# The order in which the weight-load slots of the two expert layers are given out

## The chip, the cores and the metric

The kernel runs on one core of one Trainium2 chip. The time is the device time of one execution in microseconds (us); three runs give a median, and one further execution was profiled. The engines are TensorE (PE, with its weight loads PEld), VectorE (DVE), ScalarE (ACT), GpSimd (POOL) and SyncE (SP), whose queue issues nearly all weight loads.

## The reference, cut to what matters

Two networks of two layers each run one after the other on 256 tokens of width 1024 (the first carries 256 context tokens too). Everything is float32. In the first network each layer is a mixer (attention) and then a mixture of experts with 32 experts, of which every token uses two:

```python
for l in range(2):
    x (and ctx) = x + gate * mixer_l(modulate(norm(x)))        # mixer_ab in layer 0, mixer_c in layer 1
    tokens = modulate(norm(x))           # 512 tokens in layer 0 (ctx and x), 256 in layer 1 (x alone)
    group, expert = top1(tokens @ w_group), top2(tokens @ w_expert inside that group)
    for e in range(32):                  # w1, w3: 1024 x 512; w2: 512 x 1024
        y_e = (silu(t_e @ w1[e]) * (t_e @ w3[e])) @ w2[e]      # t_e: the tokens routed to e
    x = x + gate * sum of weight_e * y_e
```

The second network (sparse and latent attention, then a plain feed-forward) follows and is untouched.

## The kernel before

`body` runs `mixer_ab`, `moe(0)`, `mixer_c`, `moe(1)` and then the second network. An expert layer (`moe`) gives every expert 64 token rows; a rare second part (`overflow`, behind a branch on the largest count, L1325) takes what is over. It works on pairs of experts, sixteen pairs: `gather` builds the transposed tokens `xp` of four experts with one-hot matrices `G` (PE writes `tp`), `up` multiplies by w1 and w3 (PE writes `mm`, all through the helper `mm` at L1024), `turn` transposes the gated product (L1248), `down` multiplies by w2, `weigh` scales (DVE, ACT, L1279 to L1281), and `scatter` adds the rows back into `x` (L1295).

All 32 experts' weights pass through SBUF once: 32 x 3 x 2 MB in each layer, as loads of 128 x 1024 floats (512 KB), 12 for each expert, 384 in a layer. Each load goes into a **slot**. `raws` (L295) asks `slot` for the next one and issues the load with `late` (L185), which keeps it in program order on SP's queue. SP works its queue strictly in order: a load that must wait for its slot's memory holds back all behind it.

Slots come from three places. The ring buffers that the mixers use for their own weights (6 `raw`, 3 `wh`, 3 `wl`, written `b` in the tables) serve as 12 slots. Tiles of the mixers that are dead by then serve as well: `r0` to `r3` are the mixer's attention output (in layer 1 the tiles `oT` that `mixer_c`'s last product reads), and `r6`, `r7` the residual rows of the context, which layer 1 no longer needs after `mixer_c`'s norm at its start. The rest is memory of the mixer's own pools, which close when it ends: `x0`, `x1`, ... at the front of that region and `y0`, `y1`, ... behind the layer's own tiles. Layer 0 has 4 x and 2 y (with 4 r and 12 b: 22 slots), layer 1 has 8 x and 5 y (31 slots). In what order they go out in a lap is a table, one string for each layer:

```python
order = order.split()
order += [k for k in (*extra, *once) if k not in order] + ["b"] * (len(base) - order.count("b"))
lap = [(k, base.pop(0) if k == "b" else extra.get(k)) for k in order]
self.rings["raw"] = [e for k, e in lap if e]
self.lap = [new.get(k) or once.get(k) or e for k, e in lap]
```

The first lap takes the entries of `self.lap`; later laps repeat the same order. In the first lap a load waits until the mixer's last access to the memory under the slot is done, in later laps until PE has read what lay in it. The mixer's end is in SP's way like this: the router's `logits` are the mixer's last step (L976 on ACT writes squares into a tile `pr` of the closing pools, L421 on POOL ends the norm's factor), and `x0` of both layers lies over memory that this step uses. The loads of the mixer's own weights (L319, `w_out_ab`, `w_out_c`; split into `wh` and `wl` at L327 and L330) stand ahead of the expert loads in SP's queue.

At the end of a layer `ahead` loads the first weights of what follows into the `raw` ring (for layer 1 three loads of `w_in_2`), before the branch L1325.

Of the kernel before, what the change touches and what calls it, by code (L numbers as in the profile page):

```python
# [25 lines left out]
def shape_constants():  # L26
# [32 lines left out]
    for dim in (64, 32):  # L59
# [21 lines left out]
PTE = "avav"  # L81

MOE = ((4, 2), (8, 5))
MJ = ("r0 r1 r2 y0 y1 x0 x1 x2 x3 b b b b r3 b b b b b b b b",
      "x0 x1 x2 x3 b b b b r0 r1 r2 r3 b b x4 x5 x6 x7 r6 r7 b b b b b b y0 y1 y2 y3 y4")
AH = ("ap", "ap")

CP = dict(s=2, tp=3, o=1, pa=2)
# [30 lines left out]
class Kern:  # L119
# [877 lines left out]
    def moe(self, l, whos, ahead=list):  # L997
# [16 lines left out]
        free |= {f"y{i}": (more, f"y{i}", 1) for i in range(MOE[l][1])}  # L1014
        self.slots(first, MOE[l][0], order=MJ[l], free=free)
        gates = []
# [948 lines left out]
```

## Time and profile before

| | |
|---|---|
| median of 3 runs | 2349.37 us (2348.11 to 2349.89) |
| profiled execution | 2353.45 us, its span 2351.7 us |
| busy in the span | PE 2181.2 us (93%), DVE 1119.8 (48%), ACT 780.7 (33%), POOL 345.9 (15%) |
| moved by DMA | 593.12 MB, mean 252 GB/s |

Busy time is that of the profiled execution's span, which leaves out 1.75 us of that execution's time. Matmuls are pipelined and their ends are modelled, so PE's busy time counts waiting inside the pipeline too. The page also cuts the span into 40 slices of 58.8 us with the busy share of each engine and the DMA rate in them; layer 0's experts lie in slices 6 to 14, layer 1's in slices 19 to 27.

### The profile page before, as it was taken

Reading aid. Unit: us, or ns where it says so; the run is one execution under the profiler, and the core shown is the slowest. Engines: PE = TensorE matmul, PEld = TensorE weight load, DVE = VectorE, ACT = ScalarE, POOL = GpSimd, SP = SyncE. Lnnn points to the kernel's source line nnn. Section 1 sums busy time; section 2 is a strip of 40 time slices with the busy share of each in tenths; the row PEclk is TensorE's granted clock in tenths of the full one; section 3 lists DMA queues with packets and bytes.
Section 4 is the critical chain, followed back from the end, with each engine's and each line's share of the span. In section 5 each row is a group of like instructions: output and inputs, shape, how many; then the busy total and the mean of one; then the engine's idle time right before and its main releaser. Section 6 shows DMA issues by size and latency. Waiting matters only on the chain. (4 is left out here: it accounts for less than half of the span.)

```text
span 2351.7 us, 32726 instructions
## 1 busy us (share of the span) xinstructions
PE 2181.2 (93%) x12405; PEld 1391.2 (59%) x12405; DVE 1119.8 (48%) x2251; ACT 780.7 (33%) x1585; POOL 345.9 (15%) x478
## 2 busy tenths in 40 slices
PE   5999989999999998998899999999899999899998
PEld 3865564444444437986433333333667998767997
DVE  4565664434343347766312122221566654666654
ACT  3444542111111115655201110110555443655443
POOL 1621120000000003443000000000323110232111
PEclk8999999999999999999899999999989999989999
DMA  8467639999999983220999999999433652425561
GB/s 290 134 226 270 220 113 367 381 387 387 387 387 386 387 303 114 77 72 9 357 387 387 386 387 387 386 387 383 152 126 116 230 178 99 160 84 169 188 207 37
DMA packets 306785, 593.12 MB, mean 252 GB/s; under 512 B 25270, under 2 KB 57020, under 8 KB 306620
## 3 DMA queue, kind: packets, MB, share of 16 engines
q1 hardware_dynamic: 305436, 587.68, 70.3%
q10 hardware_dynamic: 1184, 3.27, 0.4%
q8 instruction: 100, 1.64, 0.3%
q14 instruction: 65, 0.53, 0.1%
HBM read 589.82 MB, written 1.05 MB: 251 GB/s over the span
## 5 line engine op out<-in xcount | busy, mean ns | idle before, releaser
L330 POOL TENSOR_TENSOR wl<-raw,wh 128x1024 fp32r<-128x1024 f32 (+1 forms) x17 | 41.4, 2439 | 1148.8 <-SPq L1325 529.7
L1239 ACT ACTIVATE hs<-mm 128x512 f32<-128x512 f32 x32 | 19.1, 597 | 501.4 <-PE mm L1024 501.4
L330 DVE TENSOR_TENSOR wl<-raw,wh 128x1024 fp32r<-128x1024 f32 (+3 forms) x113 | 145.1, 1292 | 47.8 <-ACT wh L327 47.5
L1240 DVE TENSOR_TENSOR hs<-mm,hs 128x512 f32<-128x512 f32 x32 | 22.1, 691 | 297.6 <-ACT hs L1239 297.5
L1024 PE MATMUL mm<-x,xp 128*64 128x512 f32 x476 | 157.0, 601 | 4.7 <-DMA x<-in_w_dram 4.6
L1024 PE MATMUL mm<-raw,xp 128*64 128x512 f32 x464 | 149.4, 600 | 4.0 <-DMA raw<-in_w_dram 3.9
L327 ACT ACTIVATE wh<-raw 128x1024 fp32r<-128x1024 f32 (+3 forms) x113 | 115.8, 1032 | 84.2 <-PE pa L351 23.6
L1024 PE MATMUL mm<-r,xp 128*64 128x512 f32 x400 | 137.0, 601 | 4.1 <-DMA r<-in_w_dram 4.1
L1295 DVE TENSOR_TENSOR r<-tp,r 128x512 f32<-128x512 f32 x96 | 66.1, 690 | 102.3 <-PE tp L1024 102.1
L1250 ACT ACTIVATE gp<-tp 128x512 f32<-128x512 f32 x32 | 19.1, 597 | 264.4 <-PE tp L1248 264.4
L1024 PEld LDWEIGHTS tp<-G,u 128*128 128x128 f32 x768 | 97.7, 199 | 8.5 <-issue 8.5
L1024 PE MATMUL tp<-G,u 128*128 128x256 f32 x768 | 99.9, 292 | 2.7 <-DVE G L1129 2.7
L1024 PE MATMUL mm<-y,xp 128*64 128x512 f32 x264 | 98.4, 602 | 3.7 <-DMA y<-in_w_dram 3.6
L1024 PE MATMUL tp<-ys,GT 128*128 128x512 f32 x384 | 95.5, 402 | 6.4 <-DVE ys L1281 4.5
L349 PE MATMUL pa<-wh,u 128*128 128x256 f32 x320 | 92.7, 292 | 3.2 <-ACT ac L836 2.9
L351 PE MATMUL pa<-wh,u 128*128 128x256 f32 x320 | 92.7, 291 | 1.1 <-DVE u L345 1.1
L1024 PEld LDWEIGHTS tp<-ys,GT 128*128 128x128 f32 x384 | 71.4, 190 | 36.7 <-issue 13.0
L350 PE MATMUL pa<-wl,u 128*128 128x256 f32 x320 | 92.2, 289 | 0.2 <-DVE wl L330 0.2
L1882 PE MATMUL o<-u,xwl 128*128 128x256 f32 x320 | 90.7, 284 | 0.4 <-DVE xwl L330 0.4
L1024 PEld LDWEIGHTS mm<-x,xp 128*64 128x64 f32 x476 | 44.2, 136 | 79.1 <-issue 47.1
L1880 PE MATMUL o<-u,xwh 128*128 128x256 f32 x320 | 91.0, 285 | 0.0
L1881 PE MATMUL o<-u,xwh 128*128 128x256 f32 x320 | 90.8, 285 | 0.0
(516 smaller groups left out, 5463.8 us busy)
## 6 DMA issues: line engine op xcount, KB each, us to landing
raw<-in_w_dram SPq DMA_DIRECT2D x179, 512.0 KB, 10.8
x<-in_w_dram SPq DMA_DIRECT2D x172, 512.0 KB, 10.8
r<-in_w_dram SPq DMA_DIRECT2D x147, 512.0 KB, 10.8
y<-in_w_dram SPq DMA_DIRECT2D x96, 512.0 KB, 10.8
wh<-in_w_dram SPq DMA_DIRECT2D x87, 512.0 KB, 10.8
wl<-in_w_dram SPq DMA_DIRECT2D x87, 512.0 KB, 10.8
raw<-in_w_mod_dram SPq DMA_DIRECT2D x84, 512.0 KB, 5.6
xraw<-in_w_ff_dram SPq DMA_DIRECT2D x68, 512.0 KB, 4.5
```

Source lines behind the costliest of these rows:

```text
L327: nc.scalar.activation(wh, raw, AF.Copy)
L330: (nc.vector if lo == "v" else nc.gpsimd).tensor_tensor(out=wl, in0=raw, in1=wh.bitcast(F32), op=ALU.subtract)
L349: mm(o, xh, wh, start=start, stop=False)
L350: mm(o, xh, wl, start=False, stop=False)
L351: mm(o, xl, wh, start=False, stop=stop)
L1024: mm = lambda *a, **kw: pe(nc.tensor.matmul(*a, **kw))
L1239: nc.scalar.activation(sg_, H[:r, 0], AF.Silu)
L1240: tt_(out=sg_, in0=H[:r, 1], in1=sg_, op=ALU.mult)
L1295: tt_(out=x, in0=o, in1=x, op=ALU.add)
L1880: mm(p1[:, j, :], wh[:, c], h[:, k, :], start=(k == 0), stop=False)
L1881: mm(p1[:, j, :], wh[:, c], lo[:, k, :], start=False, stop=False)
L1882: mm(p1[:, j, :], wl[:, c], h[:, k, :], start=False, stop=(k == KT - 1))
```

## The change

Only the two strings of the table change. In layer 0 `x0` moves from the sixth place to the last. In layer 1 the order is rewritten: `r6 r7` first, then five x, four ring buffers, `r0 r1`, three ring buffers, the y, the remaining ring buffers, `r2 r3`, and last `x1 x2 x0`. The same slots exist at the same addresses, and each load fetches the same weights in the same sequence; only which slot takes which load differs.

```diff
-MJ = ("r0 r1 r2 y0 y1 x0 x1 x2 x3 b b b b r3 b b b b b b b b",
-      "x0 x1 x2 x3 b b b b r0 r1 r2 r3 b b x4 x5 x6 x7 r6 r7 b b b b b b y0 y1 y2 y3 y4")
+MJ = ("r0 r1 r2 y0 y1 x1 x2 x3 b b b b r3 b b b b b b b b x0",
+      "r6 r7 x3 x5 x4 x6 x7 b b b b r0 r1 b b b y0 y3 y4 y1 y2 b b b b b r2 r3 x1 x2 x0")
```

On PE, DVE and ACT the instructions stand in the same order as before with other slot names in them, and POOL's are the same. SP's queue shows the change. The first place is the start of layer 1's lap, behind `mixer_c`'s last weight load; `x`, `r` and `raw` are slots, `in_w1_dram` the experts' first weights. Before:

```order
L319 DMA raw_2604_10692<-in_w_out_c_dram 128x2x512
L319 DMA raw_2621_10748<-in_w_out_c_dram 128x2x512
L185 DMA x0_2639_10834<-in_w1_dram 128x2x512
L185 DMA x1_2640_10835<-in_w1_dram 128x2x512
L185 DMA x2_2641_10836<-in_w1_dram 128x2x512
L185 DMA x3_2642_10837<-in_w1_dram 128x2x512
L185 DMA raw_2719_11044<-in_w1_dram 128x2x512
L185 DMA raw_2720_11046<-in_w1_dram 128x2x512
```

and now:

```order
L319 DMA raw_2604_10692<-in_w_out_c_dram 128x2x512
L319 DMA raw_2621_10748<-in_w_out_c_dram 128x2x512
L185 DMA r6_2651_10846<-in_w1_dram 128x2x512
L185 DMA r7_2652_10847<-in_w1_dram 128x2x512
L185 DMA x3_2642_10837<-in_w1_dram 128x2x512
L185 DMA x5_2644_10839<-in_w1_dram 128x2x512
L185 DMA x4_2643_10838<-in_w1_dram 128x2x512
L185 DMA x6_2645_10840<-in_w1_dram 128x2x512
L185 DMA x7_2646_10841<-in_w1_dram 128x2x512
L185 DMA raw_2719_11047<-in_w1_dram 128x2x512
```

`x0` was the first expert load of the layer and is now the thirty-first, the last of the lap. That lap's end and the start of the second lap (`x0` again before, `r6` again now) are the second place. Before:

```order
L185 DMA y3_2656_10851<-in_w3_dram 128x2x512
L185 DMA y4_2657_10852<-in_w3_dram 128x2x512
L185 DMA x0_2735_11142<-in_w3_dram 128x2x512
L185 DMA x1_2745_11216<-in_w2_dram 128x2x512
L185 DMA x2_2746_11218<-in_w2_dram 128x2x512
```

and now:

```order
L185 DMA r2_2649_10844<-in_w3_dram 128x2x512
L185 DMA r3_2650_10845<-in_w3_dram 128x2x512
L185 DMA x1_2640_10835<-in_w3_dram 128x2x512
L185 DMA x2_2641_10836<-in_w3_dram 128x2x512
L185 DMA x0_2639_10834<-in_w3_dram 128x2x512
L185 DMA r6_2735_11142<-in_w3_dram 128x2x512
L185 DMA r7_2745_11216<-in_w2_dram 128x2x512
```

The thirty-second load, the first that waits for PE to have read a slot, fetches the same weights into `r6` in place of `x0`. The third place is the start of layer 0's lap, behind `mixer_ab`'s last weight load. Before:

```order
L319 DMA raw_963_3846<-in_w_out_ab_dram 128x2x512
L185 DMA r0_995_4006<-in_w1_dram 128x2x512
L185 DMA r1_996_4007<-in_w1_dram 128x2x512
L185 DMA r2_997_4008<-in_w1_dram 128x2x512
L185 DMA y0_999_4010<-in_w1_dram 128x2x512
L185 DMA y1_1000_4011<-in_w1_dram 128x2x512
L185 DMA x0_991_4002<-in_w1_dram 128x2x512
L185 DMA x1_992_4003<-in_w1_dram 128x2x512
```

and now:

```order
L319 DMA raw_963_3846<-in_w_out_ab_dram 128x2x512
L185 DMA r0_995_4006<-in_w1_dram 128x2x512
L185 DMA r1_996_4007<-in_w1_dram 128x2x512
L185 DMA r2_997_4008<-in_w1_dram 128x2x512
L185 DMA y0_999_4010<-in_w1_dram 128x2x512
L185 DMA y1_1000_4011<-in_w1_dram 128x2x512
L185 DMA x1_992_4003<-in_w1_dram 128x2x512
L185 DMA x2_993_4004<-in_w1_dram 128x2x512
```

The sixth load goes into `x1` and no longer into `x0`; the sixteen behind it each move up by one slot, and the lap's last load takes `x0`.

## Rows read from the trace of the kernel before

**Rows 1.** SP's waits over the run: us in total, times, longest.

```profile
SPq L185 <- ACT pr L976: 86.4, 2, 54.5
```

**Rows 2.** SP's timeline (start us, us, instruction): mixer_c's last loads, layer 1's first laps.

```profile
1033.11 30.33 SPq L319 DMA_DIRECT2D raw<-in_w_out_c_dram  x5
1119.57 1.90 SPq L185 DMA_DIRECT2D x<-in_w_dram  x4
...
1156.10 4.70 SPq L185 DMA_DIRECT2D x<-in_w_dram  x4
```

**Rows 3.** Stretches: length, PE, PEld, DVE, ACT, POOL; PEclk, DMA share, GB/s.

```profile
310.00:320.00 10.00, 10.00 (x56) 7.34 (x55) 5.38 (x8) 6.58 (x12) 0.00 (x0) 1.00 0.53 201
320.00:340.00 20.00, 20.00 (x128) 17.50 (x127) 8.96 (x17) 10.01 (x21) 6.42 (x11) 1.00 0.00 1
370.00:372.00 2.00, 2.00 (x12) 0.70 (x10) 2.00 (x7) 0.00 (x0) 0.00 (x0) 1.00 0.26 72
372.00:400.00 28.00, 27.03 (x124) 9.20 (x122) 8.10 (x29) 4.87 (x7) 0.00 (x0) 1.00 1.02 369
1136.54:1640.00 503.46, 476.14 (x1925) 177.99 (x1926) 104.44 (x197) 54.52 (x93) 0.00 (x0) 1.00 1.05 387
```

**Rows 4.** Loads by kind: size, median us from issue to landing.

```profile
x<-in_w_dram SPq DMA_DIRECT2D x172, 512.0 KB, 10.8
raw<-in_w_out_c_dram SPq DMA_DIRECT2D x8, 512.0 KB, 3.6
```

**Rows 5.** PE's timeline in the middle of layer 1.

```profile
1313.78 2.49 PE L1024 MATMUL mm<-x,xp 128*64 128x512 f32 x8 [0.17 <-DMA x<-in_w_dram]
1316.49 1.93 PE L1024 MATMUL mm<-x,xp 128*64 128x512 f32 x6 [0.22 <-DMA x<-in_w_dram]
```

**Rows 6.** PE's timeline as layer 1 starts.

```profile
1130.47 6.14 PE L1024 MATMUL tp<-G,u 128*128 128x256 f32 x32 [2.71 <-DVE G L1129]
1136.54 2.79 PE L1024 MATMUL mm<-x,xp 128*64 128x512 f32 x12
...
1154.65 1.94 PE L1024 MATMUL mm<-x,xp 128*64 128x512 f32 x8
1156.42 1.89 PE L1024 MATMUL mm<-r,xp 128*64 128x512 f32 x8
```

**Rows 7.** PE's group of scatter from 1136 to 1640: busy us, mean ns.

```profile
L1024 PE MATMUL tp<-ys,GT 128*128 128x512 f32 x112 | 27.5, 398 | 0.0
```

**Rows 8.** Lines in 1040 to 1120: ns min/median/max, first to last start.

```profile
L351 PE MATMUL pa<-wh,u x35: 279/281/415, 1039.8 to 1061.8; 128*128 128x256 f32 x35
L330 DVE TENSOR_TENSOR wl<-raw,wh x7: 1212/1215/2052, 1061.8 to 1094.9; 128x1024 fp32r<-128x1024 f32 x7
L888 PE MATMUL o<-vt,pt x48: 273/275/377, 1072.3 to 1104.0; 128*128 128x128 f32 x48
L351 PE MATMUL pa<-wh,r x27: 388/393/628, 1066.0 to 1114.4; 128*128 128x512 f32 x27
```

**Rows 9.** SP's timeline, layer 0's first lap and the start of its second.

```profile
306.76 2.34 SPq L185 DMA_DIRECT2D y<-in_w_dram  x2
345.19 1.90 SPq L185 DMA_DIRECT2D x<-in_w_dram  x4
...
370.35 2.08 SPq L185 DMA_DIRECT2D r<-in_w_dram  x3
```

**Rows 10.** PE's timeline as layer 0's experts start.

```profile
368.38 2.36 PE L1024 MATMUL mm<-r,xp 128*64 128x512 f32 x9
```

**Rows 11.** POOL's and DVE's timelines at the end of layer 1.

```profile
1651.38 4.13 POOL L330 TENSOR_TENSOR wl<-raw,wh 128x832 fp32r<-128x832 f32 x2 [0.16 <-ACT wh L327]
1657.58 0.69 DVE L1295 TENSOR_TENSOR r<-tp,r 128x512 f32<-128x512 f32 x1 [0.24 <-PE tp L1024]
```

**Rows 12.** The line L330 on DVE, 300 to 320 us, then 320 to 340.

```profile
L330 DVE TENSOR_TENSOR wl<-raw,wh x6: 1225/1226/1787, 301.2 to 316.6; 128x1024 fp32r<-128x1024 f32 x6
...
L330 DVE TENSOR_TENSOR wl<-raw,wh x2: 1224/1224/1225, 325.3 to 328.5; 128x1024 fp32r<-128x1024 f32 x2
```

## The prediction, made before the changed kernel ran

> **What bounds the kernel now.** I read SP's waits first. The only one on the mixer's last step stands there twice, 86.4 us in all [rows 1]. SP's timeline says where: in layer 1 SP has issued mixer_c's last load at 1033.11 + 30.33 = 1063.4 and issues the first expert load, into `x0`, at 1119.57 [rows 2]. In layer 0 it issues into `y1` until 309.1 and then nothing until `x0` at 345.19 [rows 9]. The reader is to see that SP, not the DMA engines, stands still: from 320 to 340 they move 1 GB/s [rows 3].
>
> Whether that idle time can be turned into an earlier end depends on what bounds the layer behind it. From 1136.54 to 1640, DMA moves 387 GB/s at a share of 1.05 [rows 3]: layer 1 is bound by its weights. One load of 524,288 bytes takes 0.524 / 0.387 = 1.355 us there. In the middle of the layer PE waits for `x` loads, and its two-slot groups stand 1316.49 - 1313.78 = 2.71 us apart, two loads' time [rows 5]. A load lands 10.8 us after its issue in the crowded queue, 8 x 1.355, so eight are under way; in mixer_c, where loads were sparse, 3.6 us [rows 4].
>
> PE's own need is smaller. Where all weights lie ready, two slots take 1156.42 - 1154.65 = 1.77 us, so 0.885 each [rows 6]. For 384 slots that is 340 us, 8 gathers of 6.14 make 49 [rows 6], the scatter 27.5 [rows 7]: some 416 us, and a few more for the turns. Layer 1 lasts 503 from its first `mm`.
>
> **The change, layer 1.** The sum is how far ahead of before the stream of 384 loads runs once PE begins to free slots. From then on both kernels move the same bytes at 1.355 us each.
>
> When can the first lap's 31 loads go? `r6` and `r7` are free when SP reaches them at 1063.4, and so are the five x, which lie over pools that the product from `wh` and `u` reads last at 1061.8. The ring follows as mixer_c's products and splits let go of it (`raw` until the split at 1094.9), the y after the L888 product at 1104.0, `r2`, `r3`, `x1`, `x2` and the last ring buffers after the last L351 at 1114.4 [rows 8], `x0` at 1119.57 [rows 2]. So ten loads are out by about 1071, nine more by about 1098, two at 1104, ten between 1112 and 1120. These groupings are an estimate: I followed each load's awaited access from the program to its row. The last ten need 10 x 1.355 = 13.6 us from about 1116, so the lap is full at about 1130.
>
> PE's first expert `mm` stays at 1136.54. It follows the gather of 1130.47, which waits 2.71 us for `G` on DVE [rows 6], the router's chain, and no DMA. So DMA stands idle from 1130 to the first free slot. In layer 0 that took 370.35 - 368.38 = 1.97 us from the first `mm` [rows 9, 10]; here it gives 1138.5 for the thirty-second load. The queue is empty then, so it lands as mixer_c's loads did, 3.6 us later: 1142.1. Before, that load was issued at 1156.10 [rows 2] and landed 10.8 later, 1166.9. The stream is 166.9 - 142.1 = **24.8 us** ahead.
>
> The restart may not run at full rate at once. The nearest row is layer 0's: 372 to 400 at 369 GB/s [rows 3], against 387 a loss of 28 x (1 - 369/387) = 1.3 us. Part of that is PE-paced, and here slots come free every 0.885 us against 1.355 needed, so I take 0.6, between 0 and 1.3. Layer 1: 24.8 - 0.6 = **24.2 us**. The bounds: with 10.8 us of latency in place of 3.6, and the full 1.3, 24.8 - 7.2 - 1.3 = 16.3; with a restart that costs neither the latency nor the ramp, 28.4.
>
> For the gain to survive, PE must take the other 353 loads as fast as they come: 353 x 1.355 = 478 us against its 416. It does, by 60 us.
>
> *Its end.* The last lap covers 12 slots in both (384 = 12 x 31 + 12), but the third `w_in_2` load gets its `raw` slot some two us later relative to the stream, since that slot now holds a later load. POOL's split of it ends at 1655.5 and DVE's last scatter at 1658.27 [rows 11], so 2.7 us hide it: 0, and at most 2 without that cover.
>
> **The change, layer 0.** Here 22 slots are full in both kernels before PE reads one. Before, the last 17 were issued from 345.19 on, and they had landed before the second lap could go: at 370 to 372 DMA is down to 72 GB/s [rows 3], and the first second-lap load, `r0` at 370.35, follows PE's first `mm` at 368.38 [rows 9, 10]. Issuing 16 of them in the idle time from 309 gains nothing, since the twenty-third load still waits for that read: 0, at most 0.4 for the restart. The wait of 36.1 us that SP had here ends as DMA idle time before 368.
>
> **What the moves could cost.** Early loads now run beside the mixers' tails. The nearest pair of rows is DVE's split at L330: median 1226 ns in 300 to 320, where DMA moves up to 201 GB/s, and 1224 in 320 to 340, where it moves 1 [rows 3, 12]. So 0. SP's queue past the moved loads: behind `x0` now stands only the second lap, which waits for PE anyway; mixer_c's own loads all stand ahead.
>
> **The sum.** Profiled execution 2353.45, span 2351.7, 1.75 outside. 2353.45 - 24.2 = 2329.25; that execution lies 4.1 us (0.17%) above the median of the runs, so from the median 2349.37 - 24.2 = **2325.2 us**, a gain of 1.0%. Within 0.2% (4.7 us) I call no change.
>
> **The rivals.**
>
> *PE becomes the bound.* For it: PE is busy 476.14 of the 503.46 us from 1136.54 [rows 3]. Were that all work, only 27.3 us could go, and idle time between dependent steps (a turn, a gather) would keep some 5 to 15 of it: gain 12 to 22, 2327 to 2337. Against it: a group of 8 that waits for DMA in the middle shows 2.49 us and an undisturbed one 1.94 [rows 5, 6], so busy time holds waiting, and PEld is busy 177.99 us, 35%. The Trainium skill, Perfetto Trace Analysis, section Identifying the Most-Contended Engine, says the same: matmul busy time is a bad measure of how near PE is to its roofline, and LDWEIGHTS' busy share a good one. By that rule this rival falls, and the sum stays at 24.2. Chance 12%.
>
> *Restart faster or layer 0 gains as well.* If layer 0's 17 loads were not done at 370, up to 16 x 1.355 = 21.7 us would come on top: about 2303. The 72 GB/s speak against it: 4%. Layer 1 at its bound of 28, and a little more from an earlier router: 2316 to 2320, 5%.
>
> *The order does less than it says.* Should a slot near the front be tied to the same late step (a tile of the closing pools that I took for dead), SP stands there until 1119.57 as it did at `x0`, and only the loads ahead of it are won, at 1.355 us each: behind the first `x` 2 loads, 2.7 us, 2346.7; behind the first `r` 11 loads, 14.9 us, 2334.5; from the nineteenth on nothing is lost against the forecast. What the first `raw` waits for I have from the program alone. Together 4%.
>
> *Slower.* The early 31 loads, 16 MB between 1063 and 1130, could slow mixer_c's tail, whose PE, DVE and ACT read and write the same SBUF, and with it PE's first `mm`. The tail from 1063.4 to 1119.6 is 56 us; it decides from 24.2 / 56 = 43% of slowdown. At half again its length the kernel loses 28 and gains 24: 2353. The L330 rows show 0.2%. Chance 3%.
>
> **The chances.** My forecast (gain 21 to 28, 2321 to 2328) 72%, the rivals as above. The range 2320 to 2334 takes the forecast and about two thirds of the PE rival, in all near 80%; it reaches to the bound of 28 on one side and close to that of 16 on the other. Faster 0.93, same 0.03 (an `x` at the front blocked, or a loss that just eats the gain), slower 0.04.
>
> **What would show it.** Right: SP's long wait on L976 is gone and what is left of it sits on the lap's last load; 31 loads are out between 1063 and 1120; DMA idles from about 1130 to 1138.5; from then on 387 GB/s until about 1616; layer 1's last scatter at about 1634 in place of 1657.6, layer 0's end unchanged, the first `mm` of both layers at 368.4 and 1136.5. Wrong: a new stall of SP before the thirty-first load, a first `mm` that comes later, PE groups in the middle of layer 1 that no longer wait for DMA, or a rate below 380 after 1150.

## The result, and the profile after

The changed kernel takes 2325.54 us (median of 4 runs, 2322.87 to 2326.82), the kernel before 2349.63 us beside it (4 runs). The ratio is 0.9896, 95% interval 0.9879 to 0.9913: 24.1 us or 1.0% faster. Forecast were 2325.2 and a range from 2320 to 2334.

SP's waits of the changed kernel (us in total, times, longest) answer to [rows 1].

```profile
SPq L185 <- PE mm L1024: 164.2, 193, 24.7
...
SPq L185 <- ACT pr L976: 1.7, 1, 1.7
```

The 86.4 us on the mixer's last step are gone but for 1.7. In their place SP's longest wait on the experts' matmuls is 24.7 us; SP's timeline says where that one lies.

```profile
344.21 0.37 SPq L185 DMA_DIRECT2D x<-in_w_dram  x1
369.33 2.08 SPq L185 DMA_DIRECT2D r<-in_w_dram  x3
...
1059.66 0.98 SPq L185 DMA_DIRECT2D r<-in_w_dram  x2
1060.73 2.63 SPq L185 DMA_DIRECT2D x<-in_w_dram  x5
1063.45 24.99 SPq L185 DMA_DIRECT2D raw<-in_w_dram  x4
...
1093.70 7.76 SPq L185 DMA_DIRECT2D y<-in_w_dram  x5
1108.31 2.81 SPq L185 DMA_DIRECT2D wh<-in_w_dram  x2
...
1114.25 1.98 SPq L185 DMA_DIRECT2D x<-in_w_dram  x3
1134.50 0.88 SPq L185 DMA_DIRECT2D r<-in_w_dram  x2
```

In layer 0 the last load of the lap, `x0`, goes out at 344.21, and the first of the second lap at 369.33, against 370.35 before [rows 9]: SP waits the 24.7 us there, for PE's first read. In layer 1 the 31 loads go out between 1059.66 and 1116.23, and the thirty-second at 1134.50, where before it went at 1156.10 [rows 2]. PE's timeline as layer 1 starts, and DVE's row of the last scatter, show what that is measured from and to.

```profile
1126.86 5.75 PE L1024 MATMUL tp<-G,u 128*128 128x256 f32 x32 [2.71 <-DVE G L1129]
1132.54 1.94 PE L1024 MATMUL mm<-r,xp 128*64 128x512 f32 x8
...
1629.09 0.69 DVE L1295 TENSOR_TENSOR r<-tp,r 128x512 f32<-128x512 f32 x1 [0.23 <-PE tp L1024]
```

From the first `mm` to the start of the last scatter layer 1 takes 1629.09 - 1132.54 = 496.6 us; before it took 1657.58 - 1136.54 = 521.0 [rows 6, 11]. That is 24.5 us, the whole gain of the medians. The two spans differ by more, 28.3 us (2351.7 and 2323.4); the rest lies ahead of layer 1's first `mm`, which comes 4.0 us earlier in this execution. The experiments below show that such shifts occur with either order.

The stretches (length, PE, PEld, DVE, ACT, POOL; PEclk, DMA share, GB/s) answer to [rows 3].

```profile
320.00:340.00 20.00, 20.00 (x130) 17.50 (x130) 9.57 (x17) 10.03 (x22) 7.39 (x12) 1.00 0.66 237
340.00:368.00 28.00, 13.43 (x92) 12.66 (x93) 21.43 (x72) 7.48 (x14) 4.02 (x4) 0.63 0.19 66
...
1130.00:1136.50 6.50, 6.50 (x39) 3.92 (x40) 4.44 (x17) 2.24 (x4) 0.00 (x0) 0.95 0.13 29
1136.50:1142.00 5.50, 5.50 (x28) 1.78 (x26) 0.52 (x2) 1.93 (x3) 0.00 (x0) 1.00 0.97 349
...
1142.00:1616.00 474.00, 452.06 (x1894) 170.85 (x1892) 101.77 (x182) 52.20 (x90) 0.00 (x0) 1.00 1.05 387
```

In layer 0 the loads have only moved: DMA is now busy from 320 to 340, where it stood at 1 GB/s, and idles later instead (66 GB/s from 340 to 368). In layer 1 the lap is full before PE starts (29 GB/s from 1130 to 1136.5), DMA restarts behind the first read and then runs at the same 387 GB/s as before.

### The profile page after: what moved, and what is told of

It is laid out like the page before. It is cut to its first block, busy times and chain, and to the rows that moved or that the text cites. A ratio compares the mean times of both kernels' runs of the same rounds, so it can differ in the third digit from the quotient of the medians.

```text
span 2323.4 us, 32736 instructions
## 1 busy us (share of the span) xinstructions
PE 2159.5 (93%) x12405; PEld 1383.1 (60%) x12405; DVE 1119.2 (48%) x2251; ACT 781.2 (34%) x1585; POOL 346.4 (15%) x478
## 5 line engine op out<-in xcount | busy, mean ns | idle before, releaser
L330 POOL TENSOR_TENSOR wl<-raw,wh 128x1024 fp32r<-128x1024 f32 (+1 forms) x17 | 41.4, 2442 | 1123.4 <-ACT wh L327 553.9
L330 DVE TENSOR_TENSOR wl<-raw,wh 128x1024 fp32r<-128x1024 f32 (+3 forms) x113 | 145.0, 1291 | 46.3 <-ACT wh L327 45.7
L1024 PE MATMUL mm<-raw,xp 128*64 128x512 f32 x480 | 154.8, 599 | 3.8 <-DMA raw<-in_w_dram 3.8
L1024 PE MATMUL mm<-x,xp 128*64 128x512 f32 x452 | 148.9, 600 | 4.0 <-DMA x<-in_w_dram 4.0
L1024 PE MATMUL mm<-r,xp 128*64 128x512 f32 x400 | 145.8, 601 | 3.7 <-DMA r<-in_w_dram 3.7
L1024 PEld LDWEIGHTS mm<-raw,xp 128*64 128x64 f32 x480 | 44.5, 136 | 74.9 <-issue 48.2
```

What stands on the lines that cost most here:

```text
L330: (nc.vector if lo == "v" else nc.gpsimd).tensor_tensor(out=wl, in0=raw, in1=wh.bitcast(F32), op=ALU.subtract)
L1024: mm = lambda *a, **kw: pe(nc.tensor.matmul(*a, **kw))
```

## The experiments

The theory under test: **the gain is the lead of the load stream when PE begins to free slots**, 1.355 us for each load that lies in SBUF by then and did not before; in layer 0 that number is 22 in both orders. Rivals are named with each run. One cut serves all: stretch A is layer 0 from the first `mm` to the start of the last scatter, B from there to layer 1's first `mm` (mixer_c and the router), C layer 1 from its first `mm` to the start of its last scatter. Worked out from the DVE and PE rows of each profile, in us:

| kernel | median | ratio to before, interval | A | B | C |
|---|---|---|---|---|---|
| before | 2349.6 | | 515.7 | 252.4 | 521.0 |
| changed | 2325.5 | 0.9896 (0.9879 to 0.9913) | 514.9 | 250.3 | 496.6 |
| l0_only | 2346.6 | 0.9996 (0.9983 to 1.0009) | 516.0 | 249.9 | 520.5 |
| l1_only | 2323.8 | 0.9902 (0.9886 to 0.9918) | 515.5 | 251.9 | 496.7 |
| x0_last | 2343.0 | 0.9985 (0.9976 to 0.9993) | 515.6 | 252.2 | 516.1 |
| coarse | 2325.4 | 0.9907 (0.9893 to 0.9921) | 515.4 | 251.3 | 496.8 |
| x0_at3 | 2344.6 | 0.9981 (0.9971 to 0.9992) | 514.7 | 250.3 | 519.2 |
| x0_at12 | 2334.2 | 0.9945 (0.9926 to 0.9964) | 515.4 | 250.8 | 504.9 |
| x0_at19 | 2325.5 | 0.9901 (0.9883 to 0.9918) | 515.6 | 252.5 | 496.7 |
| drop7 | 2335.9 | 0.9944 (0.9927 to 0.9961) | 516.1 | 253.2 | 507.0 |
| l0_drop7 | 2335.4 | 0.9948 (0.9933 to 0.9964) | 524.9 | 252.2 | 496.4 |
| l1_rows1 | 2327.9 | 0.9913 (0.9899 to 0.9927) | 515.2 | 250.3 | 498.5 |
| l1_33 | 2330.2 | 0.9918 (0.9906 to 0.9931) | 515.8 | 255.0 | 497.7 |
| both_more | 2325.3 | 0.9895 (0.9880 to 0.9910) | 513.5 | 254.2 | 498.0 |

The runs of before beside them had medians of 2347.7 (l0_only to coarse), 2348.7 (x0_at3 to drop7) and 2349.9 (the last four). Where all that a kernel leaves alone stays the same, A differs by 1.3 us, C by under 1, and B by up to 3.3 between profiles. The second network behind C, whose instructions no kernel changes, takes from 689.9 to 696.7 us, so the difference of two profiles' spans says little about a change. The expectations start from the first runs, 2349.6 and 2325.5; where the runs of before beside a kernel lie lower, a median can leave its range by as much without saying anything of the theory, and the ratio and C decide.

**Each layer's order alone.** One of the two strings is put back.

```diff
 # l0_only: layer 1 as before
-      "r6 r7 x3 x5 x4 x6 x7 b b b b r0 r1 b b b y0 y3 y4 y1 y2 b b b b b r2 r3 x1 x2 x0")
+      "x0 x1 x2 x3 b b b b r0 r1 r2 r3 b b x4 x5 x6 x7 r6 r7 b b b b b b y0 y1 y2 y3 y4")
 # l1_only: layer 0 as before
-MJ = ("r0 r1 r2 y0 y1 x1 x2 x3 b b b b r3 b b b b b b b b x0",
+MJ = ("r0 r1 r2 y0 y1 x0 x1 x2 x3 b b b b r3 b b b b b b b b",
```

> Layer 0 has the new order, layer 1 the one of before. Theory (lead of the stream): layer 0's second lap waits for PE's first read in both orders, so the time is that of before, 2349.6 within 2 us; in the profile DMA moves loads from 309 to 345 and then idles, and the first second-lap load goes out 2 us behind the first mm. Rival (both layers gain): the profiled execution of the changed kernel was 1.8 us ahead of the one of before by the end of layer 0's experts and 4.0 us ahead at layer 1's first mm; if that is the order's doing, 2346 to 2348, and layer 1's first mm near 1132.5.

> Layer 1 has the new order, layer 0 the one of before. Theory (lead of the stream): the whole gain, 2325.5 within 2 us; from the first mm of layer 1 to its last scatter 497.3 us as in the changed kernel, against 521.7 before. Rival (both layers gain): 2327 to 2329, since layer 0's part is missing, and layer 1's first mm back at 1136.5.

Layer 0's order is worth nothing that the runs can tell (0.9996; the interval leaves room for up to 4 us), layer 1's the whole gain (0.9902, beside 0.9896 for both). The median of l0_only, 2346.6, lies 1.1 us under the range given and where the rival put it, but the runs of before beside it lie 1.9 lower too, and A, where a gain of layer 0 has to show, is 516.0 against 515.7. The first `mm` of layer 1 did come at 1132.1, as the rival said; in l1_only it came at 1135.8, and the gain was whole. (The 497.3 and 521.7 expected there reach to the end of the last scatter, 0.7 us more than C.) The 4.0 us by which the changed kernel's profile starts layer 1 earlier are 1.0 ahead of layer 0's experts, 0.8 in A and 2.1 in B. The eight kernels here with layer 0's new order show B from 249.9 to 253.2, which takes in the 251.9 and 252.4 of the two with the old one: an effect of the order on B is not shown.

**Which part of layer 1's order counts.** In x0_last `x0` alone is taken to the end of the order of before; in coarse the five late slots are.

```diff
 # x0_last, coarse: in place of layer 1's string
-      "x0 x1 x2 x3 b b b b r0 r1 r2 r3 b b x4 x5 x6 x7 r6 r7 b b b b b b y0 y1 y2 y3 y4")
+      "x1 x2 x3 b b b b r0 r1 r2 r3 b b x4 x5 x6 x7 r6 r7 b b b b b b y0 y1 y2 y3 y4 x0")
+      "x3 b b b b r0 r1 b b x4 x5 x6 x7 r6 r7 b b b b b b y0 y1 y2 y3 y4 r2 r3 x1 x2 x0")
```

> Layer 0 new; in layer 1 the order of before with x0 alone moved to the end. Theory: SP now stands at x1 until the last L351 product has been read, about 1115.6 in place of 1119.6, so the stream is 4 us ahead: 2345.6, 2344 to 2347. Rival (x0 alone was the block, the rest of the order is decoration): about 2326.

> Layer 0 new; in layer 1 the order of before with only x0, x1, x2, r2 and r3 taken to the end. SP stands at the fourth ring buffer from 1071 to 1092 and at the eighth from about 1096 to 1112, with 16 loads out by then. Theory: the last 15 need 15 x 1.355 = 20 us from 1112, so the lap is full at about 1135, ahead of the first freed slot at 1138.5, and nothing is lost: 2325.5, 2323 to 2328. Rival (every slot must be asked for when it comes free): SP's two stands of 21 and 16 us cost a good part of the gain, 2330 to 2340.

SP's waits and its timeline in x0_last:

```profile
SPq L185 <- DVE pr L923: 52.1, 1, 52.1
...
1113.46 1.40 SPq L185 DMA_DIRECT2D x<-in_w_dram  x3
```

The wait has not gone, it has changed its partner: 52.1 us on DVE's L923 in place of 54.5 on ACT's L976 [rows 1]. The first load stands 1134.42 - 1113.46 = 21.0 us ahead of the first `mm` against 17.0 before (1136.54 - 1119.57), 4.0 more, and C is 4.9 shorter. The median lies 1.0 below the range given, and 4.7 under that of the runs of before beside it (by the ratio's interval 1.6 to 5.6); the rival's 2326 is out. coarse shows the other end. SP's timeline there:

```profile
1101.28 14.93 SPq L185 DMA_DIRECT2D wh<-in_w_dram  x3
1116.25 2.24 SPq L185 DMA_DIRECT2D wl<-in_w_dram  x3
```

SP stands for most of 14.93 us within the three `wh` loads, and nothing is lost (C 496.8): the lap is still full before PE frees a slot.

**x0 at the third, twelfth and nineteenth place.** The changed order with `x0` moved forward.

```diff
 # x0_at3, x0_at12, x0_at19: in place of layer 1's string
-      "r6 r7 x3 x5 x4 x6 x7 b b b b r0 r1 b b b y0 y3 y4 y1 y2 b b b b b r2 r3 x1 x2 x0")
+      "r6 r7 x0 x3 x5 x4 x6 x7 b b b b r0 r1 b b b y0 y3 y4 y1 y2 b b b b b r2 r3 x1 x2")
+      "r6 r7 x3 x5 x4 x6 x7 b b b b x0 r0 r1 b b b y0 y3 y4 y1 y2 b b b b b r2 r3 x1 x2")
+      "r6 r7 x3 x5 x4 x6 x7 b b b b r0 r1 b b b y0 y3 x0 y4 y1 y2 b b b b b r2 r3 x1 x2")
```

> The changed kernel with x0 of layer 1 as third load, behind r6 and r7. Theory: x0 is issued at 1119.6 as before and two loads are won, 2 x 1.355 = 2.7 us: 2346.9, 2345 to 2349. Rival (early loads that are not many are worth what they are in the changed kernel, since the lap goes on in a better order): well below 2340.

> The changed kernel with x0 of layer 1 as twelfth load. Theory: eleven loads are won, 11 x 1.355 = 14.9 us: 2334.7, 2332 to 2337; the thirty-second load lands at about 1123.2 + 20 x 1.355 = 1150.3. Rival (PE, not the stream, sets the end): nothing lost against the changed kernel, 2325.5.

> The changed kernel with x0 of layer 1 as nineteenth load. Theory: thirteen loads are left when x0 goes out at 1119.6; the lap is full at about 1139.5 and the thirty-second load would land at 1140.8, before the 1142.1 that the first freed slot allows, so nothing is lost though SP stands some 15 us at x0: 2325.5, 2323 to 2328. Rival (each place of x0 ahead of the end costs 1.355 us): 12 x 1.355 = 16 us lost, 2341.

C is shorter than before's by 1.8, 16.2 and 24.4 us, where 2.7, 14.9 and 24.2 were expected; the medians fall in the three ranges but for x0_at3, which is 0.4 under its own. SP's timeline of x0_at12 and then of x0_at19:

```profile
1115.49 0.37 SPq L185 DMA_DIRECT2D x<-in_w_dram  x1
...
1136.94 1.94 SPq L185 DMA_DIRECT2D r<-in_w_dram  x2
```

```profile
1099.59 0.88 SPq L185 DMA_DIRECT2D y<-in_w_dram  x2
1121.68 0.37 SPq L185 DMA_DIRECT2D x<-in_w_dram  x1
...
1140.63 0.88 SPq L185 DMA_DIRECT2D r<-in_w_dram  x2
```

With `x0` nineteenth SP stands still for 21.2 us (1100.47 to 1121.68), and the second lap starts at 1140.63, 2.0 us behind its first `mm` at 1138.7, as in the changed kernel: nothing is lost, and the rival's rate per place fails. With `x0` twelfth it starts at 1136.94, 4.6 us behind a first `mm` at 1132.3, while DMA moves 386 GB/s from 1130 to 1134: the queue, still full of the first lap, holds it, not PE.

**Fewer slots.** Seven slots of a layer are left out of its lap, with their memory still allocated so that nothing else moves.

```diff
+            drop = [k[1:] for k in order.split() if k[0] == "-"]
...
-            lap = [(k, base.pop(0) if k == "b" else extra.get(k)) for k in order]
+            lap = [(k, base.pop(0) if k == "b" else extra.get(k)) for k in order if k not in drop]
 # drop7: -y0 -y1 -y2 -y3 -y4 -r2 -r3 in layer 1; l0_drop7: -y0 -y1 -x0 -x1 -x2 -x3 -r3 in layer 0
```

> The changed kernel without seven of layer 1's slots (y0 to y4, r2, r3; their memory stays allocated and unused), so a lap of 24. Theory: the lead is what lies in SBUF when PE starts, so seven loads less cost 7 x 1.355 = 9.5 us: 2335.0, 2332 to 2338, with the same first mm. Rival (PE is the bound of the layer now): nothing lost, 2325.5. Rival (fewer slots also starve the queue of its eight loads under way): more than 15 us lost.

> The changed kernel without seven of layer 0's slots (y0, y1, x0 to x3, r3; their memory stays allocated and unused), a lap of 15. The question is why layer 0 gained nothing. Theory (its stream starts at PE's first read in both orders, and what lies in SBUF by then is its lead): seven loads less cost 7 x 1.355 = 9.5 us, 2335.0 (2332 to 2338), first mm to last scatter of layer 0 about 524.5 in place of 515. Rival (PE is the bound of layer 0, busy for 97 to 100% of it, and a lead is worth nothing there): 2325.5, and 515 unchanged.

Both cost what seven loads take: C is 10.5 us longer in drop7, and A 10.0 longer in l0_drop7 (9.5 expected), with the medians at 2335.9 and 2335.4. The loss arises at the start and not along the layer: from 1200 to 1600 drop7 moves 386 to 387 GB/s like the others, so the rival of a queue that starves for slots is out. The last scatter of layer 0 in l0_drop7, and its stretch from 400 to 500 (columns as above):

```profile
L1296 DVE TENSOR_TENSOR r<-tp,r x64: 674/692/692, 453.5 to 890.3; 128x512 f32<-128x512 f32 x64
...
400.00:500.00 100.00, 98.38 (x486) 46.04 (x482) 41.84 (x85) 17.23 (x31) 0.00 (x0) 1.00 1.04 384
```

PE is busy for 98.38 of these 100 us and yet 10 us can be lost to loads: layer 0 too follows its stream. It did not gain from the new order because no more loads lay in SBUF when PE started, not because PE had no room.

**More slots.** To try the theory upward, layer 1 scatters each pair by itself, so that single buffers give memory back (l1_rows1); two slots more use it (l1_33); both_more does the same in both layers, with 24 and 33 slots.

```diff
-            gt = self.t(wk, [P, T], F32R, tag="GT", bufs=2)[:r]
+            gt = self.t(wk, [P, T], F32R, tag="GT", bufs=NT // 2)[:r]
...
-                hi, lo = (self.t(wk, [P, 512], F32R, tag=f"ys{n}{a}", bufs=2)[:r] for a in range(2))
+                hi, lo = (self.t(wk, [P, 512], F32R, tag=f"ys{n}{a}", bufs=NT // 2)[:r] for a in range(2))
...
-                two, rows = (rows, []) if p % 2 else ([], rows)
+                two, rows = (rows, []) if p % 2 or NT == 2 else ([], rows)
...
+                if p == 16 and NT == 2:
+                    scatter(rows)
+                    rows = []
 # l1_33 besides: y5 y6 behind y2, MOE = ((4, 2), (8, 7))
```

> Control for the next kernel, with the 31 slots of the changed kernel: in layer 1 each pair's rows are added into x by themselves (no longer two pairs at a time), with one buffer each for ys and GT. The same matmuls, 32 more additions of 0.69 us on DVE, which has work for a fifth of the layer. Theory: no change while the stream sets the pace, 2325.5 (2323 to 2328), 496.6 us from layer 1's first mm to its last scatter. Rival (PE stands at the single buffers): 2 us or more slower.

> The control with two more slots in layer 1 (y5, y6, in the memory that the single buffers give back), a lap of 33. Theory: DMA idles from the lap's end to the first freed slot, so two more loads fit there, 2 x 1.355 = 2.7 us faster than the control: 2322.8 (2320 to 2326), 493.9 us from first mm to last scatter. Rival (y5, y6 come free late, or the first gather now waits for memory of the moved pool): no gain, or a later first mm.

> The same in both layers: single buffers, 24 slots in layer 0 and 33 in layer 1. Theory: 2.7 us from each layer, 2320.1 (2317 to 2324). Rival (layer 0's PE, busy 97 to 100%, has no room for a faster stream, or for scattering each pair by itself): 2322.8 or slower, with layer 0's 515 us unchanged or longer.

Here the expectation failed as to the end. The medians of l1_33 and both_more, 2330.2 and 2325.3, lie above their ranges; that of the control, 2327.9, lies in its own, but 2.3 us above the changed kernel, as its rival had it (the intervals of the two ratios overlap), and its C is 1.9 us longer. SP's timeline at the end of layer 1, of l1_rows1 and then of l1_33, shows when the first load of the next stage goes out, which stands behind the last expert load:

```profile
1611.55 6.38 SPq L185 DMA_DIRECT2D raw<-in_w_in_dram  x3
```

```profile
1613.04 3.28 SPq L185 DMA_DIRECT2D raw<-in_w_in_dram  x3
```

From the first `mm` (1134.8 and 1139.3) that is 476.8 and 473.7 us: the stream is 3.0 us ahead, as two more slots should make it (2.7). But from there to the last scatter l1_33 takes 24.0 us (to 1637.0), the control 21.7 (to 1633.3), the changed kernel 20.0 (from 1609.12). So of the 3.0 us C keeps 0.8 against the control. PE's timeline of l1_33, after the last weights:

```profile
1624.80 2.25 PE L1024 MATMUL tp<-ys,GT 128*128 128x512 f32 x8
1631.93 2.47 PE L1024 MATMUL tp<-ys,GT 128*128 128x512 f32 x5 [4.88 <-DVE GT L1267]
1635.35 1.65 PE L1024 MATMUL tp<-ys,GT 128*128 128x512 f32 x3 [0.95 <-DVE ys L1281]
```

With one `GT` the matrix of the last pair cannot be built while the pair before still reads it, and the last scatter waits 4.88 us for it. In the control, with the same single buffer, it waits less:

```profile
1628.15 2.47 PE L1024 MATMUL tp<-ys,GT 128*128 128x512 f32 x5 [3.10 <-DVE GT L1267]
```

So the buffer is not what sets the two apart. The 1.78 us between the waits are one subtraction that stands ahead of `GT` in DVE's order, of l1_33 and then of the control:

```profile
1627.37 2.46 DVE L1281 TENSOR_TENSOR ys<-gs,ys 128x512 fp32r<-128x512 f32 x1
```

```profile
1625.38 0.68 DVE L1281 TENSOR_TENSOR ys<-gs,ys 128x512 fp32r<-128x512 f32 x1
```

both_more shows 2.46 us there too; what slows it was not tested. B is also at its longest in the two kernels with 33 slots, 255.0 and 254.2, where others show 249.9 to 253.2. Whether the memory that the added slots push along does that was not settled; the granted clock has a part in it (last section). both_more has a shorter A (513.5, where two slots should give 2.7 and gave about 2), loses it again in B and C, and is no better than the changed kernel (2325.3).

## Why the prediction was right, point by point

- **What bounds the layer.** Layer 1 still moves 387 GB/s from 1142 to 1616, and a layer takes 10.5 us (layer 1) or 10.0 us (layer 0) more when seven of its slots are missing. Shown.
- **The lead of 24.8, less 0.6.** C is 24.5 us shorter in the changed kernel and 24.4 in l1_only. The places of `x0` bear out both the price of a load and the point from which a late slot is free. But the two small terms were mis-sized, and that 24.2 was met within 0.3 us is in part luck. Counted along SP's timeline, the 98th load goes out 109.0 us behind the first `mm` before and 86.6 us now: a lead of 22.4. In l1_only, coarse, x0_at19 and l0_drop7 it is 22.2 to 23.2. So the restart took 1.6 to 2.6 us of the 24.8, where the prediction put 0.6 and at most 1.3. The rest came back later: by the first load of the next stage (rows below, before and now) the lead is (1636.97 - 1136.54) - (1609.12 - 1132.54) = 23.85 us, and the last 0.6 are won behind the stream. The 1.4 between is within what the stream varies by: its way from the 98th load to the 384th takes 390.0 us in before but 389.3 in l0_only, with the same order, and 388.6 in the changed kernel but 389.5 in l1_only.

```profile
1636.97 4.21 SPq L185 DMA_DIRECT2D raw<-in_w_in_dram  x3
```

```profile
1609.12 6.38 SPq L185 DMA_DIRECT2D raw<-in_w_in_dram  x3
```

- **The restart.** The thirty-second load went out 1.96 us behind the first `mm` (1134.50 - 1132.54; 1.97 forecast). Each clock reading of the layer was forecast some 4 us late, as the whole of layer 1 stood earlier in that execution; the differences hold.
- **When the lap is full.** The last two y were out by 1101.5 (forecast 1104), the last ten loads went out from 1108.3 to 1116.2 (1112 to 1120), and DMA moved 29 GB/s from 1130. The estimate was good, less the same 4 us, and it had room: coarse has more loads left behind the late release and loses nothing.
- **Layer 0 at 0.** Right in the result (0.9996) and for the reason given: the wait moved to PE's first read.
- **The end at 0.** POOL's last split of the changed kernel (the row below: start, us) ends at 1627.02, and the last scatter at 1629.78: the cover is 2.8 us, as before [rows 11]. The third `raw` load came 2.2 us later relative to the first, as forecast, and cost nothing; the way from the first of them to the last scatter is even 0.6 us shorter (20.6 before, 20.0 now).

```profile
1620.77 6.25 POOL L330 TENSOR_TENSOR wl<-raw,wh 128x832 fp32r<-128x832 f32 x3 [505.26 <-ACT wh L327]
```

- **Rivals.** PE as the bound is out: C shrank by the whole lead. The rule of the Trainium skill weighed there (Perfetto Trace Analysis, section Identifying the Most-Contended Engine), that matmul busy time is a bad measure of how near PE is to its roofline, agrees with layer 0 of l0_drop7, where PE at 98% busy, PEld at 46%, hid 10 us of dependence on the loads. The order doing less than it says: SP's wait on L976 shrank from 86.4 to 1.7. Slower: B in the six kernels that send nearly all the early loads of layer 1 beside mixer_c with 31 slots or fewer and the memory as it was (changed, l1_only, coarse, x0_at19, drop7, l0_drop7) is 250.3 to 253.2, mean 251.9, and in the four that keep the stall near the front (before, l0_only, x0_last, x0_at3) 249.9 to 252.4, mean 251.2. The difference is 0.7 us, within the spread of B, where 24.2 was needed.

## What to carry to other kernels

In a queue that works strictly in order, the first late slot decides for all behind it; moving only the worst one hands the stall to the next. What loads ahead are worth, in a stage that its loads bound, is (loads that lie ready when the consumer starts) x (time of one load), less what the restart costs, and once all slots are full by then, a finer order is worth nothing: first look whether the transfers have idle time between the full lap and the first read. Price the tail before paying for slots with its buffers.

## What the runs showed that was not expected

B, the same instructions each time but for the loads beside them, took 249.9 to 255.0 us between profiles, and the first `mm` of layer 0 came between 365.4 and 370.9. TensorE's clock is granted differently in stretches of mixer_c: here stretches of l1_33, then of the changed kernel, around mixer_c's last product (columns as above):

```profile
1100.00:1109.50 9.50, 4.65 (x23) 3.28 (x22) 3.71 (x9) 2.71 (x11) 2.78 (x5) 0.74 1.00 352
1109.50:1114.50 5.00, 4.94 (x12) 3.80 (x12) 0.43 (x1) 1.11 (x4) 0.00 (x0) 0.50 0.76 284
```

```profile
1100.00:1104.00 4.00, 0.93 (x7) 0.55 (x5) 0.99 (x3) 1.01 (x4) 0.74 (x2) 0.92 1.02 374
1104.00:1108.00 4.00, 4.00 (x12) 3.10 (x12) 0.32 (x1) 0.96 (x3) 0.00 (x0) 0.65 0.37 140
1108.00:1112.00 4.00, 3.22 (x20) 2.45 (x18) 3.15 (x5) 0.72 (x2) 0.00 (x0) 1.00 0.40 140
1113.60:1119.00 5.40, 5.40 (x26) 5.00 (x25) 3.99 (x5) 2.49 (x4) 1.64 (x5) 0.50 1.02 383
```

Both stand at 0.50, the lower of the two levels (1.2 GHz), in the last product, and both again in the router behind it, but not for the same time. l1_33 falls within the first stretch shown, in which PE was busy for 4.65 of 9.5 us, and does most of the product at 0.50. The changed kernel has 0.50 for a part of it (0.65 from 1104 to 1108), 1.00 from 1108 to 1112, and 0.50 again from 1113.6 on. Over the whole of B the mean granted clock goes with its length: 0.932 in l0_only (249.9 us, the shortest), 0.925 to 0.926 in eight kernels (250.3 to 252.5), 0.919 to 0.920 in five (251.9 to 255.0; the two with 33 slots are among them). As the ranges overlap, the clock is a part of B's spread and not all of it, and no run changes it alone.
